# A feed-forward block whose up projection takes seven block products for eight, whose inner layer goes through DRAM, and whose down projection is a stage of its own

## The chip, the cores and the metric

One Trainium2 chip, of which the kernel uses one core. The metric is the device time of one execution in microseconds (us); shorter is better. Engines are named as in the profile: PE (matrix products), PEld (PE's weight loads, which overlap them), DVE, ACT and POOL (the three elementwise engines) and SP, whose queue issues nearly every DMA transfer.

## The reference

A whole decoder layer for 1024 tokens of 1024 channels, in float32. The change concerns its last part, a gated feed-forward block with 2816 = 22 x 128 inner channels:

```
h = rms_norm(x, pre_ffn_norm[l])
u = causal_dwconv(h @ ffn_w_up[l], ffn_conv_w[l], ffn_conv_b[l])     # 2 * 2816 columns, width 3
gate, val = jnp.split(u, 2, axis=-1)
f = (jax.nn.gelu(gate, approximate=True) * val) @ ffn_w_down[l]
x = x + rms_norm(f, post_ffn_norm[l])
```

The two products are [1024 x 1024] @ [1024 x 5632] and [1024 x 2816] @ [2816 x 1024].

## The kernel before

Everything is held with channels on the 128 partitions and tokens along the free axis, in two halves of 512 tokens. Every operand of a product is split exactly into a high and a low part (`hi`, `lo`), and each product is made of three matmuls: hi by hi, hi by lo, lo by hi. One matmul is 128x128 by 128x512. A weight tile of 128 output channels ("unit", 128x1024 for the up projection) is loaded by `load_w` (L264-271): the raw tile comes by DMA (L267), ACT makes `whi` (L269), POOL makes `wlo` (L270). `fm_unit` (L273) runs a unit, half by half: 8 blocks of 128 channels x 3 matmuls = 24 matmuls a half into one PSUM bank ("dense"; six banks).

`up(f)` (L1325-1348) makes one tile f of the inner layer from two units, u = 2f (gate) and 2f+1 (value). `conv` (L300-309) takes each bank out of PSUM: ACT writes bias + tap 0 (L303), DVE adds two shifted taps from PSUM (L307), and for the second half of the tokens two small halo operations (128x1 and 128x2, L309) bring in the last two columns of the first half (kept by a copy, L305). ACT applies gelu to the gate (L1338), DVE multiplies by the value (L1345), ACT and DVE split the result (L1346, L1347); it stays in SBUF as `mhi`, `mlo`. `down` (L1350-1360) multiplies chunks of four (one of two) inner tiles by the down weights and adds up `acc` in SBUF (L1356 on ACT for the first chunk, L1358 on DVE after). Chunks of the up projection and of the down projection alternate. The first four tiles run by halves (N_FIRST), since the second half of the tokens is still being normalised in the stage before (output projection and norms, L1264-1316). The last chunk goes by pieces of tokens, each normalised and stored at once (L1418-1441); for it x1 is loaded again in 16 transfers of 256 KB (L1387). The gelu uses another ACT table than the norms, so a table load stands behind the last gelu (L1379).

The order on each engine's queue is set by a list scheduler at build time. An engine takes its queue strictly in this order.

Of the kernel before, what the change touches and what calls it, by code (L numbers as in the profile page):

```python
# [1457 lines left out]
```

## Time and profile before

| | us |
|---|---|
| median of 3 runs (lowest to highest) | 2350.91 (2350.25 to 2351.12) |
| span of the profiled execution | 2347.0 |
| PE busy | 2261.6 |
| DVE busy | 1311.3 |
| ACT busy | 1055.4 |
| POOL busy | 912.3 |

The times are those of whole executions, the span that of the work inside one profiled execution; the difference between median and span is 3.9 us. Busy times of PE overlap: one matmul's record lasts 0.39 us, but the next one starts 0.23 us after it, so on PE the cadence of starts is the cost and not the mean record. A pause of PE shows as a value in square brackets ahead of the instruction that follows, with what ended it.

### The profile page before, as it was taken

How to read it: one execution, taken by the hardware profiler on the slowest of the kernel's cores; microseconds unless marked ns; L12 is line 12 of the kernel's file. 1: busy time of each engine (PE TensorE's matmuls, PEld its weight loads, DVE VectorE, ACT ScalarE, POOL GpSimd, SP SyncE). 2: the span in 40 equal slices, each digit the busy share in tenths (PEclk: the TensorE clock that was granted, in tenths of full speed). 3: DMA queues.
4: the chain of work that ended last, by engine and by line, in shares of the span. 5: the costliest groups of instructions: out<-in, count | busy, mean ns of one | idle time of the engine just before them, and what ended most of it. 6: DMA issues, size and time to landing. Idle time of an engine off the chain costs nothing.

```text
span 2347.0 us, 29315 instructions
## 1 busy us (share of the span) xinstructions
PE 2261.6 (96%) x11020; PEld 1828.0 (78%) x11020; DVE 1311.3 (56%) x2351; ACT 1055.4 (45%) x1842; POOL 912.3 (39%) x671
## 2 busy tenths in 40 slices
PE   8999999999999999999998999998999999999997
PEld 7997666667887788778786888876788888888886
DVE  8324875781476676565757443378714343443556
ACT  7144665666466766444443322345433131322334
POOL 4122565565233324553535264455422221222213
PEclk9999999999999999999999999998999999999998
DMA  5233112101111112021212462343221111112132
GB/s 191 81 88 96 48 40 69 57 8 59 37 54 46 46 45 72 32 77 41 77 53 83 159 202 97 117 152 111 78 63 41 59 41 50 54 32 67 46 117 72
DMA packets 90126, 173.49 MB, mean 74 GB/s; under 512 B 25280, under 2 KB 39296, under 8 KB 89984
## 3 DMA queue, kind: packets, MB, share of 16 engines
q1 hardware_dynamic: 89696, 171.39, 22.4%
q8 instruction: 87, 1.43, 0.2%
q14 instruction: 55, 0.45, 0.1%
q10 hardware_dynamic: 288, 0.22, 0.0%
HBM read 138.55 MB, written 33.03 MB: 73 GB/s over the span
## 4 chain that ended last, share of the span: by engine, by line
PE 82%; DVE 11%; ACT 3%; issue 2%; POOL 2%; DMA 1%; SPq 0%; DVEq 0%; ACTq 0%; POOLq 0%
PE dense L205 66%; PE ps_s L205 5%; PE ps_o L205 4%; PE ps_t L205 4%; PE ps_b L205 2%; DVE mx L813 2%; POOL wlo L270 1%; DVE row L307 1%; DVE o L1306 1%; ACT whi L269 0%; DVE acc L1410 0%; POOL R L1116 0%; DVE xe L1138 0%; POOL osq L1278 0%; DVE cp L733 0%
## 5 line engine op out<-in xcount | busy, mean ns | idle before, releaser
L270 POOL TENSOR_TENSOR wlo<-wraw,whi 128x1024 fp32r<-128x1024 f32 (+2 forms) x194 | 405.5, 2092 | 837.1 <-ACT whi L269 799.7
L205 PE MATMUL dense<-h_hi,whi 128*128 128x512 f32 x992 | 401.6, 405 | 3.5 <-DVE row L307 3.4
L205 PE MATMUL dense<-h_lo,whi 128*128 128x512 f32 x992 | 393.4, 397 | 0.0
L205 PE MATMUL dense<-h_hi,wlo 128*128 128x512 f32 x992 | 392.0, 395 | 0.0
L269 ACT ACTIVATE whi<-wraw 128x1024 fp32r<-128x1024 f32 (+2 forms) x194 | 179.2, 925 | 386.0 <-PE dense L205 350.2
L205 PE MATMUL dense<-hi,whi 128*128 128x512 f32 x832 | 326.6, 393 | 11.2 <-ACT whi L269 11.2
L205 PE MATMUL dense<-hi,wlo 128*128 128x512 f32 x832 | 327.0, 394 | 4.4 <-POOL wlo L270 4.3
L205 PE MATMUL dense<-lo,whi 128*128 128x512 f32 x832 | 326.0, 392 | 1.5 <-POOL lo L1313 1.5
L205 PEld LDWEIGHTS dense<-h_hi,whi 128*128 128x128 f32 x992 | 188.3, 190 | 44.4 <-ACT sa L1026 3.6
L205 PEld LDWEIGHTS dense<-h_hi,wlo 128*128 128x128 f32 x992 | 187.6, 189 | 40.0 <-issue 1.1
L205 PEld LDWEIGHTS dense<-h_lo,whi 128*128 128x128 f32 x992 | 188.3, 190 | 36.0 <-issue 1.8
L307 DVE SCALAR_TENSOR_TENSOR u<-dense,pv,u 128x511 f32<-128x511 f32 (+1 forms) x176 | 130.8, 743 | 133.3 <-ACT u L303 132.0
L853 POOL TENSOR_TENSOR wT_lo<-wT,wT_hi 128x512 fp32r<-128x512 f32 x132 | 169.2, 1292 | 86.7 <-ACT wT_hi L852 80.2
L205 PEld LDWEIGHTS dense<-hi,whi 128*128 128x128 f32 x832 | 157.5, 189 | 46.2 <-ACT whi L269 13.4
L205 PEld LDWEIGHTS dense<-hi,wlo 128*128 128x128 f32 x832 | 157.4, 189 | 40.6 <-POOL wlo L270 7.2
L205 PEld LDWEIGHTS dense<-lo,whi 128*128 128x128 f32 x832 | 157.4, 189 | 35.3 <-POOL lo L1313 2.4
L205 PE MATMUL dense<-mhi,whi 128*128 128x512 f32 x288 | 112.2, 392 | 0.3
L205 PE MATMUL dense<-mlo,whi 128*128 128x512 f32 x288 | 112.3, 390 | 0.0
L1043 POOL TENSOR_TENSOR s_lo<-sa,s_hi 128x512 fp32r<-128x512 f32 (+2 forms) x48 | 53.8, 1125 | 148.9 <-ACT s_hi L1042 137.6
L842 ACT ACTIVATE wT<-ps_s 128x512 f32<-128x512 f32 x132 | 78.4, 594 | 68.3 <-PE ps_s L205 63.6
L205 PE MATMUL dense<-mhi,wlo 128*128 128x512 f32 x288 | 105.6, 389 | 0.0
L813 DVE TENSOR_REDUCE mx<-ps_t 128x1 f32<-128x384 f32 (+3 forms) x192 | 93.9, 514 | 18.1 <-PE ps_t L205 15.9
(377 smaller groups left out, 4560.8 us busy)
## 6 DMA issues: line engine op xcount, KB each, us to landing
wraw<-in_wfm SPq DMA_DIRECT2D x62, 512.0 KB, 3.4
wraw<-in_wup SPq DMA_DIRECT2D x52, 512.0 KB, 3.3
g_d<-gate_e SPq DMA_DIRECT2D x48, 256.0 KB, 2.1
...
wraw<-in_wdn SPq DMA_DIRECT2D x32, 256.0 KB, 2.6
...
x<-in_xT SPq DMA_DIRECT2D x16, 256.0 KB, 5.5
```

Source lines behind the costliest of these rows:

```text
L205: i = f(*a, **k)
L269: act(hi, raw, AF.Copy)
L270: (V if tiles else P).tensor_tensor(lo, raw, fl(hi), op=OP.subtract)
L307: V.scalar_tensor_tensor(o[:, d:], ps[:, :512 - d], taps[d], o[:, d:], op0=OP.mult, op1=OP.add)
L813: V.tensor_reduce(mx[:, h, a, n:n + 1], pm[:, :w], axis=AX, op=OP.max)
L842: act(w.rearrange("p h q -> p (h q)"), pz, AF.Exp)
L853: P.tensor_tensor(lo, wf, fl(hi), op=OP.subtract)
L1043: (P if SB_SLO else V).tensor_tensor(s_lo[:, c0:], a[:, c0:], fl(s_hi[:, c0:]), op=OP.subtract)
L1306: i = V.scalar_tensor_tensor(o[:, j, :], o[:, j, :], pvc(PV_FFN, j), r, op0=OP.mult, op1=OP.mult)
```

## The change

The up projection keeps the first four tiles as they were, by halves. For each of the other 18 tiles, `up_pair(f)` replaces two units x two halves by a 2x2 block scheme with seven products: the contraction is cut into two halves of 512 channels (four blocks), the output into (gate unit, value unit) and the columns into the two halves of the tokens. Seven products of 4 blocks x 3 matmuls take the place of eight, 84 matmuls for 96. The token-side sums are made once (`combos`, on DVE, in place over the rows of the output projection, which are now single tiles `x`), then split into high and low parts. The weight-side sums are made for every pair in `weights7`, on POOL, and split by ACT and POOL. Results are put together in PSUM banks x, y, z with copies ("snaps") that ACT takes of unfinished sums, and additions on DVE (L1416, L1426) and POOL (L1424).

The gated inner layer is stored to DRAM (`m_d`, L1399). After the last pair the down projection runs as a stage of its own: `m_split` loads a tile (L1467), ACT and DVE split it (L1473, L1474), and five chunks follow one another. x1 is loaded by two transfers of 2 MB. The output goes out by one transfer for each tile and piece (24 for 8). Comments were emptied too, which changes nothing that runs.

```diff
-U_BUFS = 6
+U_BUFS = 4
     def lo_t(dt=R32):
-        return mp.tile([128, 512], dt, name="lo", bufs=17)
+        return mp.tile([128, 512], dt, name="lo", bufs=16)
...
+    def weights7(src0, src1, n):
+        raws = []
+        for m, src in enumerate((src0, src1)):
+            raw = (wx if turn[0] % 3 == 2 else E.wp).tile([128, 1024], F32, name="wraw", bufs=1 + (turn[0] % 3 < 2))[:, :2 * n]
+            turn[0] += 1
+            nc.sync.dma_start(raw, src)
+            raws.append(raw)
+        a11, a12, a21, a22 = [r[:, s] for r in raws for s in (slice(0, n), slice(n, 2 * n))]
...
+        act(whi, raws[0], AF.Copy)
+        P.tensor_tensor(wlo, raws[0], fl(whi), op=OP.subtract)
...
+        P.tensor_tensor(u1, a21, a22, op=OP.add)
+        P.tensor_tensor(u2, u1, a11, op=OP.add)
+        P.tensor_tensor(u4, u2, a12, op=OP.add)
+        act(h24, f24, AF.Copy)
+        P.tensor_tensor(l24, f24, fl(h24), op=OP.subtract)
+        P.tensor_tensor(u3, a11, a21, op=OP.add)
+        act(h31, f31, AF.Copy)
+        P.tensor_tensor(l31, f31, fl(h31), op=OP.subtract)
+        act(ahi, a22, AF.Copy)
+        P.tensor_tensor(alo, a22, fl(ahi), op=OP.subtract)
...
+    def snap(ps):
+        s = up_.tile([128, 512], F32, name="snap", bufs=5)
+        act(s, ps, AF.Copy)
+        return s
+    def combos(b11, b12, b21, b22, eng):
+        eng.tensor_tensor(b22, b12, b22, op=OP.subtract)
+        eng.tensor_tensor(b12, b11, b12, op=OP.subtract)
+        eng.tensor_tensor(b11, b22, b11, op=OP.subtract)
+        eng.tensor_tensor(b21, b11, b21, op=OP.add)
...
+    def gated(f, h, st):
+        V.tensor_tensor(st[0, h], st[0, h], st[1, h], op=OP.mult)
+        nc.sync.dma_start(m_d[f * 128:(f + 1) * 128, hs(h)], st[0, h])
...
+    def up_pair(f, rhs):
+        st = {}
+        w = weights7(A["wup"][2 * f], A["wup"][2 * f + 1], 512)
+        x, y, z = bank(), bank(), bank()
+        product(x, w, rhs, 1, True)
+        s1 = snap(x)
+        product(y, w, rhs, 2, True)
+        V.tensor_tensor(y, y, s1, op=OP.add)
+        conv(2 * f, 0, y, st)
+        product(x, w, rhs, 6, False)
+        s2 = snap(x)
+        product(z, w, rhs, 7, True)
+        s7 = snap(z)
+        product(x, w, rhs, 5, False)
+        s3 = snap(x)
+        P.tensor_tensor(s7, s7, s3, op=OP.subtract)
+        product(z, w, rhs, 4, False)
+        V.tensor_tensor(z, z, s2, op=OP.subtract)
+        conv(2 * f + 1, 0, z, st)
+        gated(f, 0, st)
+        product(x, w, rhs, 3, False)
+        conv(2 * f + 1, 1, s7, st)
+        conv(2 * f, 1, x, st)
+        gated(f, 1, st)
...
+    for q, k, t, place in sorted(later, key=lambda x: (-x[0], x[1])):
+        rhs[q][k] = hi, lo = place(), x_t()
+        act(hi, t, AF.Copy)
+        V.tensor_tensor(lo, t, fl(hi), op=OP.subtract)
+    for f in range(N_FIRST, NFF):
+        up_pair(f, rhs)
...
+    def m_split(f, h):
+        src = m_tile(f, h, f % 2)
+        hi, lo = hi_t(), lo_t()
+        act(hi, src, AF.Copy)
+        V.tensor_tensor(lo, src, fl(hi), op=OP.subtract)
...
+    x1s = [x1p.tile([128, 8, 512], F32, name=f"x1_{h}") for h in range(2)]
     for h in range(2):
-            nc.sync.dma_start(x1s[j][h], E.x1_d[j * 128:(j + 1) * 128, hs(h)])
+        nc.sync.dma_start(x1s[h], E.x1_d[:, hs(h)].rearrange("(a p) t -> p a t", p=128))
```

Three places of the queues matter below. The first is POOL in the middle of the up projection. Before, it holds one kind of work there, `wlo` of the next unit:

```order
L270 TENSOR_TENSOR wlo_17117<-wraw_17114,whi_17116 128x1024
L270 TENSOR_TENSOR wlo_17193<-wraw_17190,whi_17192 128x512
L270 TENSOR_TENSOR wlo_17227<-wraw_17224,whi_17226 128x512
L270 TENSOR_TENSOR wlo_17261<-wraw_17258,whi_17260 128x512
L270 TENSOR_TENSOR wlo_17295<-wraw_17292,whi_17294 128x512
```

Now one pair puts nine operations there (`uf0` and `uf1` hold u3, u1 and u2, u4; `uhi`, `ulo` their parts; `ahi`, `alo` those of one quarter of the weights; the two snaps are s7 and s3):

```order
L1349 TENSOR_TENSOR uf0_16958<-wraw_16950 128x512
L1354 TENSOR_TENSOR uf0_16958<-wraw_16948,wraw_16950 128x512
L1344 TENSOR_TENSOR wlo_17107<-wraw_17102,whi_17106 128x1024
L1350 TENSOR_TENSOR uf1_16959<-uf0_16958,wraw_16948 128x512
L1351 TENSOR_TENSOR uf1_16959<-uf1_16959,wraw_16948 128x512
L1353 TENSOR_TENSOR ulo_16963<-uf1_16959,uhi_16962 128x1024
L1424 TENSOR_TENSOR snap_16883<-snap_16883,snap_16897 128x512
L1358 TENSOR_TENSOR alo_16955<-wraw_16950,ahi_16954 128x512
L1356 TENSOR_TENSOR ulo_16961<-uf0_16958,uhi_16960 128x1024
```

Six of them are 128x512 and three 128x1024, and all read and write SBUF.

The second is ACT, in the same stretch. Before, gelu (L1338) follows the conv of its own half, and nothing behind it is wanted by the running product but the next `whi`:

```order
L303 ACTIVATE u0_18617<-dense_18618,pv_65 128x512
L1338 ACTIVATE u0_18617<-u0_18617 128x512
L269 ACTIVATE whi_18758<-wraw_18756 128x1024
L303 ACTIVATE u0_18648<-dense_18649,pv_65 128x512
L1338 ACTIVATE u0_18648<-u0_18648 128x512
```

Now two gelus, of the second half of one pair (u0_16939) and of the first half of the next (u0_17005), stand ahead of the snap of z (snap_17037, s7) that the next pair's product 4 waits for:

```order
L302 ACTIVATE u0_16939<-dense_16820,pv_65 128x512
L302 ACTIVATE u0_17005<-dense_16975,pv_65 128x512
L1343 ACTIVATE whi_17260<-wraw_17256 128x1024
L1376 ACTIVATE snap_17023<-dense_16974 128x512
L1395 ACTIVATE u0_16939<-u0_16939 128x512
L1395 ACTIVATE u0_17005<-u0_17005 128x512
L1376 ACTIVATE snap_17037<-dense_16976 128x512
```

The gelus themselves wait for DVE's taps, so a snap now waits for DVE by way of the queue. DVE's queue up to the second of them is:

```order
L1426 TENSOR_TENSOR dense_16822<-dense_16822,snap_16869 128x512
L304 COPY halo_16913<-dense_16822 128x2
L306 SCALAR_TENSOR_TENSOR u1_16914<-dense_16822,pv_65,u1_16914 128x511
L306 SCALAR_TENSOR_TENSOR u1_16933<-snap_16883,pv_65,u1_16933 128x511
L308 SCALAR_TENSOR_TENSOR u1_16933<-halo_16913,pv_65,u1_16933 128x1
L306 SCALAR_TENSOR_TENSOR u1_16914<-dense_16822,pv_65,u1_16914 128x510
L306 SCALAR_TENSOR_TENSOR u1_16933<-snap_16883,pv_65,u1_16933 128x510
L308 SCALAR_TENSOR_TENSOR u1_16933<-halo_16913,pv_65,u1_16933 128x2
L1398 TENSOR_TENSOR u0_16851<-u0_16851,u1_16914 128x512
...
L306 SCALAR_TENSOR_TENSOR u0_17005<-dense_16975,pv_65,u0_17005 128x510
```

Between the last two shown stand the taps of u0_16939 (two from PSUM and two from its halo), a halo copy and the first tap of u0_17005.

The third place is SP's queue where the up projection ends. Before, x1 comes in pieces of 128x512 between loads of weights:

```order
L267 DMA wraw_19279<-in_wdn4 128x256
L1387 DMA hi_19419<-x1_d_73 128x512
L1387 DMA hi_19423<-x1_d_73 128x512
L1387 DMA lo_19420<-x1_d_73 128x512
L267 DMA wraw_19307<-in_wdn4 128x256
```

Now each half of x1 is one transfer, and the first one stands ahead of the loads of the inner layer's tile 0 (u0_18351, u0_18357), the second ahead of tiles 2 and 3:

```order
L1467 DMA u1_18363<-m_d_14865 128x512
L1467 DMA u1_18369<-m_d_14865 128x512
L1517 DMA x1_0_19931<-x1_d_73 128x8x512
L1467 DMA u0_18351<-m_d_14865 128x512
L1467 DMA u0_18357<-m_d_14865 128x512
L1517 DMA x1_1_19932<-x1_d_73 128x8x512
L266 DMA snap_19905<-in_wdn5 128x512
L1399 DMA m_d_14865<-u0_18237 128x512
L1467 DMA u1_18387<-m_d_14865 128x512
L1399 DMA m_d_14865<-u0_18325 128x512
```

On ACT the table load and the first `m_split` now stand behind the last gelu, so the down projection's first operand is made after it:

```order
L302 ACTIVATE u0_18325<-dense_18206,pv_65 128x512
L1395 ACTIVATE u0_18325<-u0_18325 128x512
L1492 ACT_TABLE_LOAD
L1473 ACTIVATE hi_18353<-u0_18351 128x512
L1473 ACTIVATE hi_18359<-u0_18357 128x512
L1473 ACTIVATE hi_18365<-u1_18363 128x512
```

Before, the table load had the last chunks of the down projection beside it:

```order
L1346 ACTIVATE mhi_19186<-u0_19086 128x512
L1379 ACT_TABLE_LOAD
L269 ACTIVATE whi_19309<-wraw_19307 128x256
L269 ACTIVATE whi_19337<-wraw_19335 128x256
```

What was behind the gelu there were weights of matmuls that had inner tiles in SBUF; now it is the inner tiles themselves.

A fourth place is the first pair. On ACT its second snap (snap_15637, s2) stands behind the gelu of its own first half:

```order
L302 ACTIVATE u0_15619<-dense_15589,pv_65 128x512
L1343 ACTIVATE whi_15874<-wraw_15870 128x1024
L1395 ACTIVATE u0_15619<-u0_15619 128x512
L1376 ACTIVATE snap_15637<-dense_15588 128x512
```

That gelu's taps stand on DVE behind eight splits of token-side sums (L1458, the first and the last of them shown) and the taps of the last unit before the pairs (u1_15474):

```order
L1458 TENSOR_TENSOR x_15531<-x_14450,hi_15530 128x512
...
L1458 TENSOR_TENSOR x_15559<-x_14049,lo_15558 128x512
L306 SCALAR_TENSOR_TENSOR u1_15474<-dense_15449,pv_65,u1_15474 128x511
L308 SCALAR_TENSOR_TENSOR u1_15474<-halo_15166,pv_65,u1_15474 128x1
L306 SCALAR_TENSOR_TENSOR u1_15474<-dense_15449,pv_65,u1_15474 128x510
L308 SCALAR_TENSOR_TENSOR u1_15474<-halo_15166,pv_65,u1_15474 128x2
L1416 TENSOR_TENSOR dense_15589<-dense_15589,snap_15603 128x512
L1398 TENSOR_TENSOR u0_15436<-u0_15436,u1_15474 128x512
L304 COPY halo_15618<-dense_15589 128x2
L306 SCALAR_TENSOR_TENSOR u0_15619<-dense_15589,pv_65,u0_15619 128x511
L306 SCALAR_TENSOR_TENSOR u0_15619<-dense_15589,pv_65,u0_15619 128x510
```

Before there was nothing of this kind: the units with both halves simply follow the four tiles that run by halves.

PE's queue in a steady pair D, with E the pair after it, is (product, and its number of matmuls): 6 of D 12, 7 of D 2, 1 of E 12, 2 of E 9, 7 of D 10, 5 of D 12, 2 of E 3, 4 of D 12, 3 of D 12; 84 in all. In the whole program PE has 216 matmuls fewer (18 pairs x 12), all of the form 128x128 by 128x512.

## Rows read from the trace of the kernel before

**Rows 1.** The page, first part: busy time of each engine, its share of the span, instructions.

```profile
PE 2261.6 (96%) x11020; PEld 1828.0 (78%) x11020; DVE 1311.3 (56%) x2351; ACT 1055.4 (45%) x1842; POOL 912.3 (39%) x671
```

**Rows 2.** Busy time by stretch: start and end in us, length, then busy us and instructions of each engine, TensorE's granted clock, DMA share and GB/s. The FFN fills 1700 to 2280 and has its first tiles ahead of that.

```profile
1500.00:1600.00 100.00, 91.79 (x384) 73.15 (x383) 68.02 (x58) 45.89 (x70) 53.25 (x23) 0.97 0.38 133
1600.00:1700.00 100.00, 91.06 (x376) 71.45 (x375) 81.62 (x107) 48.99 (x69) 49.09 (x22) 0.97 0.30 100
1700.00:2200.00 500.00, 499.73 (x2201) 412.79 (x2200) 190.85 (x315) 140.05 (x196) 115.37 (x62) 1.00 0.16 50
2280.00:2347.00 67.00, 51.87 (x327) 46.34 (x325) 42.32 (x90) 27.20 (x58) 18.96 (x20) 0.90 0.18 64
```

**Rows 3.** Groups of instructions between 1700 and 2200 us, POOL: line, engine, operation, tiles, shapes and count, then busy us and mean ns of one, then the idle time before and what ended it.

```profile
L270 POOL TENSOR_TENSOR wlo<-wraw,whi 128x1024 fp32r<-128x1024 f32 x32 | 76.8, 2399 | 234.0 <-ACT whi L269 234.0
L270 POOL TENSOR_TENSOR wlo<-wraw,whi 128x512 fp32r<-128x512 f32 x30 | 38.6, 1292 | 154.0 <-ACT whi L269 154.0
```

**Rows 4.** The same view and stretch, ACT.

```profile
L303 ACT ACTIVATE u<-dense,pv 128x512 f32<-128x512 f32 x60 | 46.1, 768 | 31.6 <-PE dense L205 31.6
L269 ACT ACTIVATE whi<-wraw 128x1024 fp32r<-128x1024 f32 x32 | 34.0, 1061 | 71.9 <-PE dense L205 71.9
L1338 ACT ACTIVATE u<-u 128x512 f32<-128x512 f32 x30 | 19.0, 633 | 63.8 <-DVE u L309 37.9 <-DVE u L307 25.9
L269 ACT ACTIVATE whi<-wraw 128x512 fp32r<-128x512 f32 x30 | 18.6, 630 | 94.9 <-PE dense L205 94.9
L1356 ACT ACTIVATE acc<-dense 128x512 f32<-128x512 f32 x15 | 8.8, 589 | 16.6 <-PE dense L205 16.6
```

**Rows 5.** The same view and stretch, DVE. L307 and L305 read PSUM, L1358 one operand of PSUM and one of SBUF, the others SBUF alone.

```profile
L307 DVE SCALAR_TENSOR_TENSOR u<-dense,pv,u 128x511 f32<-128x511 f32 x60 | 44.7, 745 | 102.4 <-ACT u L303 102.4
L1358 DVE TENSOR_TENSOR acc<-acc,dense 128x512 f32<-128x512 f32 x48 | 32.7, 687 | 88.6 <-PE dense L205 88.6
L309 DVE SCALAR_TENSOR_TENSOR u<-halo,pv,u 128x1 f32<-128x1 f32 x30 | 28.3, 943 | 0.0
L1345 DVE TENSOR_TENSOR u<-u,u 128x512 f32<-128x512 f32 x29 | 20.1, 692 | 1.0
L309 DVE SCALAR_TENSOR_TENSOR u<-halo,pv,u 128x2 f32<-128x2 f32 x29 | 6.0, 206 | 0.0
L305 DVE COPY halo<-dense 128x2 f32<-128x2 f32 x30 | 4.8, 159 | 98.6 <-ACT u L303 98.6
```

**Rows 6.** The timeline between 1880 and 1884 us, POOL and DVE: start, duration, engine, line, operation, tiles, and in brackets the idle time before with what ended it.

```profile
1880.88 2.40 POOL L270 TENSOR_TENSOR wlo<-wraw,whi 128x1024 fp32r<-128x1024 f32 x1 [8.49 <-ACT whi L269]
...
1881.50 0.75 DVE L307 SCALAR_TENSOR_TENSOR u<-dense,pv,u 128x511 f32<-128x511 f32 x1 [4.16 <-ACT u L303]
...
1882.17 1.13 DVE L309 SCALAR_TENSOR_TENSOR u<-halo,pv,u 128x1 f32<-128x1 f32 x1
...
1883.22 0.74 DVE L307 SCALAR_TENSOR_TENSOR u<-dense,pv,u 128x510 f32<-128x510 f32 x1
```

**Rows 7.** Groups between 1480 and 1700 us, where DVE and POOL both work on SBUF: the POOL operations and one of DVE's splits.

```profile
L1315 DVE TENSOR_TENSOR lo<-o,hi 128x512 fp32r<-128x512 f32 x8 | 9.0, 1129 | 0.0
...
L1300 POOL TENSOR_TENSOR o<-o,ox 128x512 f32<-128x512 f32 x4 | 7.0, 1739 | 6.1 <-DVE o L1298 6.1
```

**Rows 8.** The timeline of PE around the pauses in the norm before the FFN. The last three rows are matmuls behind a single pause.

```profile
1585.67 0.50 PE L205 MATMUL dense<-hi,whi 128*128 128x512 f32 x1 [3.66 <-ACT whi L269]
...
1588.33 0.79 PE L205 MATMUL dense<-hi,wlo 128*128 128x512 f32 x1 [1.92 <-POOL wlo L270]
1588.92 0.63 PE L205 MATMUL dense<-hi,whi 128*128 128x512 f32 x1
...
1593.18 0.43 PE L205 MATMUL dense<-lo,whi 128*128 128x512 f32 x1
...
1649.62 0.50 PE L205 MATMUL dense<-hi,whi 128*128 128x512 f32 x1 [2.19 <-ACT whi L269]
...
1650.64 0.39 PE L205 MATMUL dense<-hi,whi 128*128 128x512 f32 x1
1650.87 0.39 PE L205 MATMUL dense<-lo,whi 128*128 128x512 f32 x1
```

**Rows 9.** Busy time by stretch once more, five microseconds in which the transfers of x1 run.

```profile
2270.00:2275.00 5.00, 5.00 (x24) 4.15 (x23) 3.60 (x6) 1.45 (x3) 1.48 (x2) 1.00 1.02 374
```

**Rows 10.** The DMA issues of the whole program: tiles, queue, number, KB each, median us from issue to landing; loads of 256 KB and those of x1.

```profile
wraw<-in_wdn SPq DMA_DIRECT2D x32, 256.0 KB, 2.6
...
hi<-x_d SPq DMA_DIRECT2D x8, 256.0 KB, 4.8
```

**Rows 11.** The timeline of ACT from 2268 to 2278 us, with the last table load and a weight split that waited for its load; and of SP, the issue of that load.

```profile
2269.32 1.28 ACT L1379 ACT_TABLE_LOAD   x1
2270.62 0.42 ACT L269 ACTIVATE whi<-wraw 128x256 fp32r<-128x256 f32 x1
...
2277.12 0.42 ACT L269 ACTIVATE whi<-wraw 128x256 fp32r<-128x256 f32 x1 [3.35 <-DMA wraw<-in_wdn]
...
2272.16 0.33 SPq L267 DMA_DIRECT2D wraw<-in_wdn  x1
```

More of the change, by code (lines that the diff above doesn't have):

```diff
@@ L1265, in tail_stage, with x_t @@
     up_ = es.enter_context(tc.tile_pool(name="up", side="right", reuse_waits="tile", bufs=U_BUFS))
+    op2 = es.enter_context(tc.tile_pool(name="o", reuse_waits="tile", bufs=1))
+    def x_t(dt=R32):
+        return op2.tile([128, 512], dt, name="x", bufs=26)
     op = ExitStack()
     ow = op.enter_context(tc.tile_pool(name="ow", reuse_waits="tile", bufs=2))
+    rows = []
     for h in range(2):
-        o = ow.tile([128, 8, 512], F32, name="o")
+        o = [x_t(F32) for _ in range(8)]
+        rows.append(o)
         def sumsq(sums, src, eng=V):
@@ new lines, in product, with bank @@
+    def product(ps, w, rhs, q, first):
+        hi, lo = w[q]
+        for k, b in enumerate(rhs[q]):
+            s = slice(k * 128, (k + 1) * 128)
+            for n, (x, y) in enumerate(((hi, b[0]), (hi, b[1]), (lo, b[0]))):
+                mm(ps, x[:, s], y, start=first and k == 0 and n == 0, stop=k == len(rhs[q]) - 1 and n == 2,
+                   skip_group_check=True)
+    def bank():
+        return psd.tile([128, 512], F32, name="dense", tag="dense")
+    def snap(ps):
+        s = up_.tile([128, 512], F32, name="snap", bufs=5)
+        act(s, ps, AF.Copy)
+        return s
@@ new lines, in combos, with conv @@
+    def combos(b11, b12, b21, b22, eng):
[3 more added lines that the diff above has]
+        eng.tensor_tensor(b21, b11, b21, op=OP.add)
+    m_d = E.scratch("m_d", [NFF * 128, T])
+    def conv(u, h, ps, st):
+        s = u % 2
+        if h == 0:
+            st["halo", s] = up_.tile([128, 4], F32, name="halo", bufs=12)
+        st[s, h] = up_.tile([128, 512], F32, name=f"u{s}")
+        E.conv(st[s, h], h, ps, [pvc(PV_FW, 3 * u + 2 - d) for d in range(3)], pvc(PV_FB, u), st["halo", s])
+        if s == 0:
+            act(st[0, h], st[0, h], AF.Gelu_apprx_tanh)
@@ new lines, in tail_stage @@
+    first = [{} for _ in range(N_FIRST)]
+    for h in range(2):
+        for f, st in enumerate(first):
+            up_half(f, h, st)
+    rhs = {q: [None] * 4 for q in range(1, 8)}
+    later = []
+    for k in range(4):
+        quarters = [(1, h2[0, k]), (2, h2[0, k + 4]), (3, h2[1, k + 4])]
+        lows = [rows[0][k], rows[1][k], rows[0][k + 4], rows[1][k + 4]]
+        combos(*lows, V)
+        for q, b in quarters:
+            rhs[q][k] = b
+        t2, t1, t4, t3 = lows
+        for q, t in ((6, t2), (7, t3)):
+            rhs[q][k] = hi, lo = x_t(), x_t()
+            act(hi, t, AF.Copy)
+            V.tensor_tensor(lo, t, fl(hi), op=OP.subtract)
+        later += [(5, k, t1, hi_t), (4, k, t4, lo_t)]
@@ new lines, in tail_stage, with w_split @@
+    for ci, (f0, nf) in enumerate(DOWN[:last]):
+        if ci == 0:
+            acc = [[x_t(F32) for _ in range(8)] for _ in range(2)]
+        down(ci, f0, nf)
+    f0, nf = DOWN[last]
+    ms = [[None, None] for _ in range(nf)]
+    ws = []
+    def w_split(j, place):
+        ws.append(load_w(A[f"wdn{last}"][j], 512, place, up_.tile([128, 512], F32, name="snap", bufs=5)))
+    for k in range(nf):
+        ms[k][0] = m_split(f0 + k, 0)
+    for j in range(4):
+        w_split(j, (x_t(), x_t()))
@@ L1390, in tail_stage @@
+    for k in range(nf):
+        ms[k][1] = m_split(f0 + k, 1)
+    for j in range(4, 8):
+        w_split(j, (hi_t(), lo_t()))
+    wx_.close()
+    x1p = es.enter_context(tc.tile_pool(name="x1", reuse_waits="tile", bufs=1))
+    x1s = [x1p.tile([128, 8, 512], F32, name=f"x1_{h}") for h in range(2)]
+    for h in range(2):
+        nc.sync.dma_start(x1s[h], E.x1_d[:, hs(h)].rearrange("(a p) t -> p a t", p=128))
     ended = None
@@ L1422, in tail_stage @@
         for j in range(8):
-            ps = psd.tile([128, 512], F32, name="dense", tag="dense")
+            ps = bank()
             hi, lo = ws[j]
```

139 lines of the change are left out of this document (59 added, 80 removed).

## The prediction

> **What bounds the kernel now.** I read the page's busy times first: PE is busy 2261.6 us of a span of 2347.0 [rows 1], so the kernel is bound by PE nearly everywhere. Then the stretches [rows 2]: from 1700 to 2200 us, inside the FFN, PE has 499.73 of 500 us at a granted clock of 1.00, and 2201 matmuls, one every 0.2272 us. DVE, ACT and POOL work for 191, 140 and 115 us of these 500. So a matmul that is taken out there saves its whole 0.2272 us, as long as the three others, with much work added, still deliver in time. The reader should keep the two stretches before in mind, 91 to 92 us of PE's 100 with DVE at 68 to 82 [rows 2]: where the work of DVE and POOL gets dense, PE does wait.
>
> **Part 1, fewer matmuls.** 216 matmuls of the form that fills the FFN go: 216 x 0.2272 = -49.1 us. A pair takes 84 x 0.2272 = 19.1 us for 21.8. This term is the surest; all others are costs.
>
> **Part 2, the work of a pair beside PE.** ACT: three splits of 128x1024 at 1.06, one of 128x512 at 0.63, four snaps at 0.59 (a copy out of PSUM), four convs at 0.77, two gelus at 0.63 [rows 4]: 3.18 + 0.63 + 2.36 + 3.07 + 1.27 = 10.5 us of 19.1. DVE: eight taps at 0.745, two additions in PSUM at 0.69, two products at 0.69, two halo copies at 0.16, four halo taps at 0.20 [rows 5]: 9.9 us of 19.1. POOL: three operations of 128x1024 at 2.40 and six of 128x512 at 1.29 [rows 3]: 14.9 us of 19.1. Taken alone, each hides beneath PE. The loads stay 1 MB a pair and the stores add 1 MB, at stretches with a DMA share of 0.16 [rows 2]; I cost them at nothing, and PE's cadence covers them unless a queue's order holds them up (part 5).
>
> DVE and POOL are not independent. A POOL operation ran from 1880.88 to 1883.28; DVE's tap from PSUM ran beside it at its normal 0.75, but the 128x1 halo tap behind it, which has its operands in SBUF, ended only at 1883.30, after 1.13 us [rows 6]. Over the stretch that form has a mean of 943 ns, while the 128x2 one, which often comes when POOL is done, has 206 [rows 5]. In the norm, POOL's 128x512 takes 1.74 for 1.29, DVE's split 1.13 for 0.69 [rows 3, 5, 7]. So operations of DVE that use only SBUF wait for POOL's to end, and the other way round. Of these a pair has eight: two taps of s7 (which is a copy in SBUF), four halo taps, two products; 1.5 + 0.8 + 1.4 = 3.7 us. POOL's 14.9 and these 3.7 together take 18.6 of 19.1 us. It fits, with half a microsecond left. The Trainium skill says the same in SBUF — State Buffer (section Who interferes with whom): DVE and GpSimd (POOL) share one pair of ports, an exclusive lock that one instruction holds to its end. By that rule the two would take turns to fill 18.6 us; the row of 1.13 us agrees.
>
> **Part 3, the chain through DVE in a steady pair.** Product 4 adds to bank z, so it has to wait for snap s7, which ACT takes only after two gelus; the second gelu wants DVE's last tap of the new pair's first half. Take T as the end of product 3 of the pair before. PE then has 60 matmuls until product 4: s7 is wanted at T + 13.6. DVE's chain begins when product 4 of the pair before ends, at T - 2.7, and goes through 16 operations: one addition (0.69), six taps (4.5), four halo taps (0.8), two halo copies (0.3), a product (0.7) and two more taps of the new half (1.5): 8.5 us. Without any waiting the gelu could start at T + 5.8 and nothing is late. But seven of them use SBUF alone. POOL's mean operation is 14.9 / 9 = 1.66 us; if each of the seven meets a working POOL, it waits between nothing and that. I take 1.07 each, some two thirds of it, since POOL's next operation is queued already when DVE's comes (7.5 in all): T + 13.3. Gelu 0.63 and snap 0.59, with some hand-over, give T + 14.65, and PE waits 1.05. One small halo tap that gets in between two POOL operations takes that away. So I count half of it, 0.55 us in 17 pairs: **+9.4** (bounds 0, and 17 x 1.05 = 18 for every pair; with all seven at the whole 1.66, T + 17.5, 5.3 us a pair, which is the rival below). A pause of this length shouldn't lower PE's cadence: one of 2.19 us was followed, a microsecond on, by starts 0.23 us apart [rows 8].
>
> **Part 4, the start of the pairs.** Eight token-side splits at 1.13 (contended) [rows 7], the last unit's taps (1.9, and 1.3 of waiting), addition, product, copy, two taps (3.0) stand on DVE ahead of the gelu that stands ahead of the first pair's snap s2. The splits can begin some 1.7 us before PE begins the pair: 9.0 + 3.2 + 3.0 - 1.7, then two gelu-length steps (1.2), say 15 us after that begin; PE wants the snap after 48 matmuls, 10.9: 4.4 us of waiting. Uncontended splits at 0.69 [as L1345 in rows 5] would give 0.9. Weight sums of the first pairs come late on ACT and POOL because both are still splitting token tiles: one ACT split with its POOL part behind is 1.06 + 2.40 = 3.5 [rows 3, 4], I take 4 for both. And pauses of 3.66 and 1.92 us were followed by some ten matmuls at 0.43 instead of 0.23 us [rows 8], +2.1. Sum **+10.5** (bounds 4 and 18).
>
> **Part 5, from up to down.** Before, chunks alternate and PE doesn't pause. Now the first chunk wants inner tiles from DRAM. Let T be the last product's end. ACT: conv 0.77, then DVE's four taps (1.9), gelu 0.63, table load 1.28 [rows 4, 5, 11]: T + 4.7, then 0.63 for the first split: T + 5.3 at least. But the loads of tile 0 stand on SP's queue behind 2 MB of x1, issued when product 4 ends, T - 2.7. In the trace, transfers of x1 filled the engines at 374 GB/s [rows 9], their own 256 KB took 4.8 for 2.6 us to land [rows 10], and a split waited 3.35 us for its load issued at 2272.16 among them, ready at 2277.1 [rows 11]: so later loads wait behind. 2 MB at 374 GB/s is 5.6 us, T + 2.9; two tiles of 256 KB 1.4, landing 2.6: T + 7. Split: PE begins at about T + 8. The second 2 MB stands ahead of tiles 2 and 3, behind tile 0: T + 4.3 + 5.6, then six transfers of 256 KB (4.2), landing and split (3.2): T + 17. PE has 24 matmuls until then, so it pauses again or runs them at the lower cadence; the other 24 of the first two units end at T + 24. Without the stage cut 48 matmuls would end at T + 10.9: **+13.5** (bounds: 6, if the transfers share and only the chain over ACT counts; 18, with the lower cadence in both pauses).
>
> **Part 6, the rest.** The first four tiles keep their matmuls and the tail its pieces; 67 us from 2280 on with 51.9 of PE [rows 2]. 24 output transfers for 8, and 128x512 tiles: nothing, at most 1 us either way.
>
> Sum, against the profiled span: 2347.0 - 49.1 + 9.4 + 10.5 + 13.5 = 2331.3, with the 3.9 us around the span 2335 us, 0.7% below 2350.9.
>
> **The rivals.** (a) The waits hide: gelus and snaps come in time in nearly every pair (0 for 9.4), the start costs 4, the cut 9: 2347 - 49.1 + 13 + 3.9 = 2315. For it: every engine alone is below 80% of a pair. Against: the port's 18.6 of 19.1. (b) Each pair waits 1.05, and start and cut stand at 14 and 18: 2347 - 49.1 + 18 + 14 + 18 + 3.9 = 2352, no change. For it: queues are taken strictly in order, and part 3 repeats identically. (c) Slower: the port between DVE and POOL becomes the bound. If POOL's operations take the contended 1.74 (and 2.84 for 128x1024 by the same 0.44 added) [rows 3, 7], they need 6 x 1.74 + 3 x 2.84 = 19.0 us, and if DVE's 3.7 come on top of that, 22.7 us a pair: 18 x (22.7 - 19.1) = 65 in the place of 9.4, so 2391. It decides the sign at 21.8 less what start and cut cost, about 20.5 us of port time a pair. Against: 0.44 is most likely just the DVE operation that POOL waited for, and then it is counted twice. (d) That the change doesn't take matmuls away is excluded: PE's queue has 216 fewer.
>
> **How the numbers follow.** Forecast 0.47, (a) 0.17, (b) 0.20, (c) 0.16. A measurement of this kernel can tell about 0.2%, 4.7 us, from no change: faster is below 2346, slower above 2356. The forecast's own bounds from parts 3 to 5 (0 to 18, 4 to 18, 6 to 18, where 33.4 is taken) give 2312 to 2356 with all ends together, which is unlikely; half of it each way is 2323 to 2346. Faster: 0.47 and 0.17 less a little = 0.63; same: 0.20; slower: 0.17. The range leaves out the end of (a) and nearly all of (c): 2313 to 2360.
>
> **What would show it.** Matmuls per pair 84 at a cadence of 0.227 between pauses; POOL 14.9 us a pair or more, with DVE's taps of s7 longer than 0.75; pauses of PE of about a microsecond ahead of product 4, ended by ACT's snap, in about half of the pairs; a pause of about 8 us at the cut, ended by a split of `m_d`, and a second; some pauses in the first pair. It would be wrong if PE pauses ahead of other products (weights from POOL late: then the port is the bound), if the granted clock drops in the pairs, or if the loads of the cut don't wait behind x1.

## The result and the profile after

The changed kernel takes 2334.43 us (median of 4 runs, 2332.65 to 2336.55) against 2350.58 for the kernel before beside it: a ratio of 0.9932, 95% interval [0.9918, 0.9946]. The prediction said 2335. The profiled span is 2331.9 us, the sum said 2331.3. But the sum is right because errors of opposite sign cancel, as the stretches show.

The page's first part and the stretches of the changed kernel (the columns as in [rows 2]):

```profile
PE 2221.6 (95%) x10804; PEld 1790.9 (77%) x10804; DVE 1415.1 (61%) x2419; ACT 1126.2 (48%) x1966; POOL 1120.3 (48%) x797
...
1600.00:1700.00 100.00, 85.78 (x340) 66.25 (x339) 89.83 (x117) 48.83 (x68) 56.19 (x23) 0.91 0.35 116
1700.00:1800.00 100.00, 94.38 (x411) 76.52 (x410) 73.92 (x89) 48.44 (x70) 85.28 (x48) 1.00 0.23 74
1800.00:2000.00 200.00, 200.00 (x884) 165.61 (x883) 138.13 (x188) 104.45 (x150) 166.43 (x95) 1.00 0.24 83
2000.00:2100.00 100.00, 84.12 (x351) 67.14 (x350) 52.73 (x79) 45.52 (x73) 41.01 (x26) 0.93 0.50 171
```

In the pairs PE is busy all the time (200.00 of 200.00), although POOL now works 83 us of 100. The pauses are at the two ends of the pairs, in the stretches from 1600 to 1800 and from 2000 to 2100 us; in two of these three the granted clock is lower too (0.91 and 0.93; 1.00 from 1700 to 1800). The timeline of PE there, matmuls that began after a pause (the bracket: length of the pause, and what ended it):

```profile
1667.75 0.79 PE L204 MATMUL dense<-hi,wlo 128*128 128x512 f32 x1 [4.96 <-POOL wlo L269]
...
1709.14 0.50 PE L204 MATMUL dense<-x,uhi 128*128 128x512 f32 x1 [1.35 <-ACT uhi L1352]
...
1722.84 0.50 PE L204 MATMUL dense<-hi,uhi 128*128 128x512 f32 x1 [1.99 <-ACT snap L1376]
...
1730.06 0.50 PE L204 MATMUL dense<-hi,uhi 128*128 128x512 f32 x1 [1.49 <-ACT snap L1376]
...
2041.12 0.50 PE L204 MATMUL dense<-hi,uhi 128*128 128x512 f32 x1 [0.23 <-ACT snap L1376]
...
2047.63 0.50 PE L204 MATMUL dense<-lo,ahi 128*128 128x512 f32 x1 [1.23 <-ACT snap L1376]
...
2063.94 2.33 PE L204 MATMUL dense<-hi,whi 128*128 128x512 f32 x4 [10.55 <-ACT hi L1473]
...
2073.92 2.08 PE L204 MATMUL dense<-hi,whi 128*128 128x512 f32 x4 [2.68 <-ACT hi L1473]
```

Between 1730.06 and 2041.12 there is none. To put a price on each stretch I cut the span at three matmuls: the last of the norm's row sums before the second half is normalised, the first product of sums (1709.14, the 263rd matmul after it; the kernel before has the same 263 there), and the last matmul of the pairs (2053.00), which only the changed kernel has. The cadence in the pairs is 0.2267 us, so 216 matmuls are 49.0 us.

| stretch | before | after | after, against before without the 216 | predicted |
|---|---|---|---|---|
| up to the last row sums | 1631.96 | 1630.92 | -1.0 | 0 |
| to the first product of sums | 67.59 | 78.22 | +10.6 | start: +10.5 |
| pairs, 1488 matmuls (337.3 at the cadence) | | 343.86 | +6.5: +4.5 in the first two, +2.0 in the last | loop: +9.4 |
| the rest, from the last product to the end | 647.44 with the pairs | 278.90 | +17.8 | cut: +13.5 |
| sum with -49.0 | 2347.0 | 2331.9 | -15.1 | -15.7 |

The third entry for "the rest" is 278.90 - (647.44 - 49.0 - 337.3). With the pauses of the first two pairs counted to the start, the start cost 15.1, the loop 2.0, and the cut 17.8. That the table has +10.6 beside +10.5 is chance: the 10.5 were forecast for waits of the first pair and its weights, most of which come behind 1709.14 or just ahead of it, and most of the 10.6 lies ahead of them.

The steady pair itself. Some groups of the changed kernel from 1740 to 2030 us (columns as in [rows 3]):

```profile
L306 DVE SCALAR_TENSOR_TENSOR u<-snap,pv,u 128x510 f32<-128x510 f32 x15 | 41.9, 2791 | 0.0
L308 DVE SCALAR_TENSOR_TENSOR u<-halo,pv,u 128x2 f32<-128x2 f32 x31 | 35.7, 1152 | 0.0
L306 DVE SCALAR_TENSOR_TENSOR u<-dense,pv,u 128x511 f32<-128x511 f32 x47 | 34.6, 737 | 0.0
L1354 POOL TENSOR_TENSOR uf<-wraw 128x512 f32<-128x512 f32 x16 | 28.0, 1747 | 0.0
L1398 DVE TENSOR_TENSOR u<-u,u 128x512 f32<-128x512 f32 x31 | 26.4, 851 | 1.9 <-ACT u L1395 0.4
L1350 POOL TENSOR_TENSOR uf<-uf,wraw 128x512 f32<-128x512 f32 x16 | 20.7, 1295 | 0.0
L308 DVE SCALAR_TENSOR_TENSOR u<-halo,pv,u 128x1 f32<-128x1 f32 x31 | 12.6, 406 | 0.0
L306 DVE SCALAR_TENSOR_TENSOR u<-snap,pv,u 128x511 f32<-128x511 f32 x15 | 11.5, 770 | 0.2 <-ACT u L302 0.2
```

Taps from PSUM keep 0.74 us. Of the operations in SBUF alone, the second tap of s7 takes 2.79 for 0.74 and the 128x2 halo tap 1.15 for 0.20, while the first tap of s7 (0.77) and the 128x1 halo (0.41) hardly wait. POOL's nine operations take 16.1 us a pair by their means, 1.2 more than the 14.9 counted.

### The profile page after: what moved, and what is told of

Its sections match the earlier page's. It is cut to its first block, busy times and chain, and to the rows that moved or that the text cites. A ratio compares the mean times of both kernels' runs of the same rounds, so it can differ in the third digit from the quotient of the medians.

```text
span 2331.9 us, 29572 instructions
## 1 busy us (share of the span) xinstructions
PE 2221.6 (95%) x10804; PEld 1790.9 (77%) x10804; DVE 1415.1 (61%) x2419; ACT 1126.2 (48%) x1966; POOL 1120.3 (48%) x797
## 3 DMA queue, kind: packets, MB, share of 16 engines
q8 instruction: 85, 1.39, 0.2%
## 4 chain that ended last, share of the span: by engine, by line
PE 78%; DVE 12%; issue 5%; ACT 2%; POOL 2%; DMA 0%; DVEq 0%; POOLq 0%; ACTq 0%
PE dense L204 62%; PE ps_s L204 6%; PE ps_o L204 4%; PE ps_t L204 4%; PE ps_b L204 2%; DVE mx L812 2%; POOL wlo L269 1%; DVE row L306 1%; DVE x L1313 1%; DVE x L1540 0%; DVE osq L1285 0%; ACT whi L268 0%; DVE xe L1137 0%; POOL wlo L1344 0%; POOL R L1115 0%
## 5 line engine op out<-in xcount | busy, mean ns | idle before, releaser
L269 POOL TENSOR_TENSOR wlo<-wraw,whi 128x1024 fp32r<-128x1024 f32 (+2 forms) x158 | 328.8, 2082 | 547.6 <-ACT whi L268 538.2
L268 ACT ACTIVATE whi<-wraw 128x1024 fp32r<-128x1024 f32 (+2 forms) x158 | 141.4, 895 | 324.6 <-PE dense L204 288.2
L204 PE MATMUL dense<-hi,whi 128*128 128x512 f32 x688 | 272.9, 399 | 24.5 <-ACT hi L1473 13.2
L204 PE MATMUL dense<-hi,wlo 128*128 128x512 f32 x688 | 268.1, 399 | 9.4 <-POOL wlo L269 8.8
L204 PE MATMUL dense<-lo,whi 128*128 128x512 f32 x688 | 271.5, 395 | 1.7 <-DVE lo L1322 0.9
L204 PEld LDWEIGHTS dense<-hi,wlo 128*128 128x128 f32 x688 | 131.5, 191 | 41.1 <-POOL wlo L269 11.5
L204 PE MATMUL dense<-x,uhi 128*128 128x512 f32 x360 | 117.0, 390 | 1.6 <-ACT uhi L1352 1.3
L306 DVE SCALAR_TENSOR_TENSOR u<-dense,pv,u 128x510 f32<-128x510 f32 (+1 forms) x140 | 101.9, 737 | 6.5 <-ACT u L302 6.4
L812 DVE TENSOR_REDUCE mx<-ps_t 128x1 f32<-128x384 f32 (+3 forms) x192 | 94.0, 514 | 18.5 <-PE ps_t L204 16.3
L1489 DVE TENSOR_TENSOR x<-x,dense 128x512 f32<-128x512 f32 x64 | 43.8, 686 | 86.7 <-PE dense L204 86.6
L851 ACT ACTIVATE wT_hi<-wT 128x512 fp32r<-128x512 f32 x132 | 82.2, 629 | 13.9 <-POOL wT L843 12.2
```

The costliest lines, as they stand in the source:

```text
L204: i = f(*a, **k)
L268: act(hi, raw, AF.Copy)
L269: (V if tiles else P).tensor_tensor(lo, raw, fl(hi), op=OP.subtract)
L306: V.scalar_tensor_tensor(o[:, d:], ps[:, :512 - d], taps[d], o[:, d:], op0=OP.mult, op1=OP.add)
L812: V.tensor_reduce(mx[:, h, a, n:n + 1], pm[:, :w], axis=AX, op=OP.max)
L851: act(hi, wf, AF.Copy)
```

## The experiments

Times are compared by their ratio to the kernel before on the same chip, and by the three stretches of the table, since the part ahead of the last row sums, at which no experiment aims, differs by up to 6 us from profile to profile (1627.4 to 1633.3). Runs without a ratio were executed once, so for them only the profile's stretches are compared.

**x1 later.** Both transfers of x1 are held behind a load of inner tiles (the last of the fourth chunk of the down projection; the expectation says the second).

```diff
+        loads.append(nc.sync.dma_start(t, m_d[f * 128:(f + 1) * 128, hs(h)]))
...
+    with tc.issue_after(loads[31].ins):
         for h in range(2):
             nc.sync.dma_start(x1s[h], ...)
```

> The two transfers of x1 are issued only behind the loads of the inner tiles of the second down chunk; nothing else changes. In the changed kernel PE pauses 10.55 us between the last product and the down projection, and the load of inner tile 0 was issued 0.4 us behind the first 2 MB of x1. Theory (loads wait behind x1): tile 0 is then issued at about the same time but lands some 2.6 us later instead of 9, its split stands ahead of the last gelu, and the pause falls to 4 to 6 us, the whole kernel by 5 to 10 us (2325 to 2330). Rival (the chain conv, taps, gelu, table load on ACT sets the restart): the pause stays above 9 us and the time within 2 us of 2334.

Ratio 0.9889 [0.9874, 0.9904], 2323.96 us. The rest fell from 278.90 to 270.8, the other stretches stayed within 0.5 us. The chain at the cut, ACT and SP of the changed kernel:

```profile
2057.57 0.63 ACT L1395 ACTIVATE u<-u 128x512 f32<-128x512 f32 x1 [3.37 <-DVE u L308]
2058.22 1.28 ACT L1492 ACT_TABLE_LOAD   x1
2063.26 2.35 ACT L1473 ACTIVATE hi<-u 128x512 fp32r<-128x512 f32 x4 [3.76 <-DMA u<-m_d]
...
2047.56 4.20 SPq L266 DMA_DIRECT2D snap<-in_wdn  x4
...
2052.80 0.38 SPq L1517 DMA_DIRECT2D x<-x_d  x1
2053.23 1.63 SPq L1467 DMA_DIRECT2D u<-m_d  x2
```

Tile 0's loads, issued 0.4 us behind x1, kept ACT waiting until 2063.26, ten microseconds, and 3.76 after the table was in. x1 itself was issued only at 2052.80, behind weight loads that SP's queue held until 2051.76. With x1 later, ACT and PE:

```profile
2056.72 2.36 ACT L1474 ACTIVATE hi<-u 128x512 fp32r<-128x512 f32 x4 [3.95 <-DMA u<-m_d]
...
2057.40 2.34 PE L204 MATMUL dense<-hi,whi 128*128 128x512 f32 x4 [5.45 <-ACT hi L1474]
```

The pause is 5.45 for 10.55, the second one (2.68) is gone, and the splits stand ahead of the last gelu and of the table load. The loads did wait behind x1; the rival is out.

**Loads first.** x1 is held as above, and the loads of the last chunk's weights are held behind inner tiles too (the last of the second chunk).

```diff
+        with tc.issue_after(loads[15].ins):
             ws.append(load_w(A[f"wdn{last}"][j], 512, place, ...))
```

> As the run with x1 later, and the loads of the last down chunk's weights too stand behind the first inner tiles, so that no other load is ahead of those on SP's queue. Theory (SP's queue in order is the whole of the cut): the first tiles are in SBUF before the last product ends, the pause falls under 2.5 us and the time by 12 to 18 us (2316 to 2322). Rival (only the 2 MB matter, the weight loads don't): as the run with x1 later, within 2 us of it. Second rival (ACT and DVE, which have the last pair's taps to do first): the pause stays at 4 us or more.

Ratio 0.9885 [0.9871, 0.9898], 2323.03 us; run again beside other kernels:

> The kernel with the first inner tiles' loads ahead of x1 and of the last weights, once more, beside the two others of this call: 2320 to 2326, about 1 us below the one with x1 later if the weight loads matter at all, a ratio to the kernel before of 0.987 to 0.990.

0.9878 [0.9864, 0.9891], 2321.77. The first inner tiles are now in SBUF in time, and PE pauses 1.39 us:

```profile
2051.15 1.48 PE L204 MATMUL dense<-hi,whi 128*128 128x512 f32 x4 [1.39 <-ACT hi L1474]
2053.73 0.80 PE L204 MATMUL dense<-lo,whi 128*128 128x512 f32 x1 [1.09 <-DVE lo L1475]
...
2067.35 0.50 PE L204 MATMUL dense<-hi,whi 128*128 128x512 f32 x1 [1.81 <-ACT whi L268]
```

(These rows are of the first run.) But the rest is 269.3 and 269.1 in the two runs, only 1.5 to 1.8 below the run with x1 later. What the first pause lost came back behind it: a split of DVE, then weights of the next units that ACT makes behind the splits. By the pause the theory was right, by the time the first rival: holding x1 back takes away some 8 of the cut's 17.8 us, the weight loads some 1.5 more.

**Eight products in the same stage.** All 18 tiles with eight products, `m_d` and the down stage kept.

```diff
-    rhs = {q: [None] * 4 for q in range(1, 8)}
...
-        up_pair(f, rhs)
...
+            w = load_w(A["wup"][u], 1024)
+            for h in range(2):
+                ps, = fm_unit(psd, w, lambda k, h: h2[h, k], 8, halves=(h,))
+                conv(u, h, ps, st)
```

> Eight products instead of seven (each unit by both halves with its whole contraction, as before), but with the inner layer in DRAM and the down projection as a stage of its own. No sums, snaps or weight sums. Theory (the 216 matmuls are worth 49 us, the start of the pairs costs some 15 and the cut some 19): the kernel before plus the cut, 2350.6 + 15 to 21 = 2365 to 2372. Rival (the cut's cost belongs to the seven products, since the last pair's chain is what delays it): 2351 to 2358.

Ratio 1.0053 [1.0039, 1.0067], 2361.47 us: between the two. Without the weight sums' buffers x1 found room early, at the beginning of the up projection, and a weight split waited for its load there (SP and ACT of that run):

```profile
1653.95 1.00 SPq L1506 DMA_DIRECT2D x<-x_d  x2
...
1668.52 1.06 ACT L268 ACTIVATE whi<-wraw 128x1024 fp32r<-128x1024 f32 x1 [6.36 <-DMA wraw<-in_wup]
```

If so, x1's transfers held up something else. With x1 behind the loads of inner tiles, as above:

> Eight products with the inner layer in DRAM and the down stage of its own, and x1's two transfers behind the loads of the second down chunk. In the run with eight products x1's transfers were issued at the beginning of the up projection and a weight load came 8 us late behind them. Theory (that pause of 3.67 us with its slow matmuls was x1's doing; the stage alone costs 5 to 6 us): 2355 to 2359, so that seven products in the same stage are worth 33 to 37 us of the 49. Rival (the pause has another cause): 2361 to 2364 as before.

1.0014 [1.0006, 1.0023], 2354.48 us, a bit under the theory's range. The stretch to the 263rd matmul is 66.53 us (74.01 with x1 early, 67.59 before), and the rest with the up projection 656.09 for 647.44: by the stretches the separate down stage costs 8.7 us with x1 behind the fourth chunk, close to the 8 that stay with seven products (269.1 - 261.1), and 5.6 in the run with x1 early (the rest there is 653.0). The pause of 3.67 us is gone, so it was x1's doing. By the profiled spans the whole kernel is 6.4 us above the kernel before, by the ratio only 0.14%, some 3 us; its executions range over 9 us.

Which kernel with seven products stands in an equal stage? The one with x1 later, 0.9889 (on another chip, against the kernel before there): 1.25%, 29 us. Beside the eight products stands the one with the loads first, 0.9878: 1.36%, 32 us, but that one holds the last weights back as well. So seven products instead of eight are worth 29 to 32 of 49.0 us in this stage, give or take some 4 by the intervals; 17 to 20 are lost, by the stretches at the two ends of the pairs.

**POOL fuller.** The split that makes l31 runs twice, or three times, in every pair.

```diff
         P.tensor_tensor(l31, f31, fl(h31), op=OP.subtract)
+        P.tensor_tensor(l31, f31, fl(h31), op=OP.subtract)
```

> The changed kernel with one more POOL operation of 128x1024 in every pair (l31 is computed twice into the same place), 2.4 us more on POOL. Theory of the prediction (POOL and DVE's SBUF-only operations fill 18.6 of 19.1 us of a shared port, so 21.0 is too much): pairs grow by 1 to 2 us, 18 to 36 in all, with pauses of PE in every pair. Rival (POOL's idle time in a pair, about a sixth in the trace of the changed kernel, some 3 us, really is room): pairs keep their 19.1 us and the span stays within 4 us of 2332.

> The same with two more POOL operations of 128x1024 in every pair, 4.8 us. Theory of a port that is full at 19.1: port time is 14.9 + 3.7 + 4.8 = 23.4 us, pairs grow by about 4.3 us, 77 in all, to a span near 2409. Rival (an idle share of 3 us is room and only the rest counts): 1.8 us a pair, 32 in all, span near 2364.

One more (executed once): a span of 2341.4 us, the pairs 352.90 for 343.86. That is outside the rival's 4 us, but not where the theory put it. In the steady pairs PE stays busy; POOL is at 95%:

```profile
1800.00:1900.00 100.00, 100.00 (x438) 81.66 (x438) 81.47 (x95) 50.97 (x71) 95.12 (x52) 1.00 0.23 79
```

A steady pair takes 19.22 us for 19.04, so some 6 of the 9 us are in the first and the last pairs. POOL's ten operations take 18.5 us a pair by their means, again 1.2 more than they need alone (14.9 + 2.4). Two more (executed once): 2401.7 us, the pairs 416.96, so 73 us more. The steady pairs take 22.7 us on average, 3.7 more; the rest is again in the first and the last ones. In every pair there is a pause of PE, as in these two, one behind the other:

```profile
1929.57 0.50 PE L204 MATMUL dense<-x,ulo 128*128 128x512 f32 x1 [2.33 <-POOL ulo L1358]
...
1952.85 0.50 PE L204 MATMUL dense<-x,ulo 128*128 128x512 f32 x1 [2.33 <-POOL ulo L1358]
```

The 73 us are near the theory's 77, but this doesn't show a full port: POOL's own eleven operations need 14.9 + 4.8 = 19.7 us, more than the 19.04 of a pair, with no DVE at all (by their means they take 21.0). Of the 3.7 us the pause is 2.33; the stretch from 1900 to 2000 us has a granted clock of 0.96 besides. What the runs do show is that a port filled to 18.6 of 19.1 us could not have taken 2.4 more for 0.2: it had more than 2 us of room, not 0.5.

**The start.** Where do the 4.96 us that PE pauses ahead of 1667.75 come from? The chain of waits of the changed kernel (start, duration, what) has one split of POOL there that takes three times its 2.40:

```profile
1660.47 7.24 POOL wlo L269
```

DVE's timeline has what ran beside it:

```profile
1660.58 0.68 DVE L1384 TENSOR_TENSOR x<-x 128x512 f32<-128x512 f32 x1
1661.19 0.68 DVE L1382 TENSOR_TENSOR x<-x 128x512 f32<-128x512 f32 x1
...
1664.20 1.28 DVE L1383 TENSOR_TENSOR x<-x 128x512 f32<-128x512 f32 x2
1665.40 0.74 DVE L306 SCALAR_TENSOR_TENSOR u<-dense,pv,u 128x511 f32<-128x511 f32 x1
1666.06 1.65 DVE L308 SCALAR_TENSOR_TENSOR u<-halo,pv,u 128x1 f32<-128x1 f32 x1
```

Eight sums and splits run in one piece, none of them waits, and POOL's split ends 2.3 us after the start of the first tap from PSUM (1665.40), about its own length; the halo tap behind that now waits in its turn. This isn't how the two always meet. In the same trace DVE runs eight splits in one piece from 1699.97 on, and POOL's operations get in between them (DVE's first four, then POOL):

```profile
1699.97 6.88 DVE L1458 TENSOR_TENSOR x<-x,hi 128x512 fp32r<-128x512 f32 x4
...
1702.87 1.73 POOL L1350 TENSOR_TENSOR uf<-uf,wraw 128x512 f32<-128x512 f32 x1
1704.57 1.74 POOL L1358 TENSOR_TENSOR alo<-wraw,ahi 128x512 fp32r<-128x512 f32 x1
```

There both take turns: 1.7 us for POOL's 1.29, and 6.88 for four splits that take 0.68 alone. What decides between the two cases no run shows. First the sums are left out:

```diff
-        combos(*lows, V)
```

> The 16 token-side sums are left out (the products take the rows as they are), so the output is not the reference's; all splits stay. Theory (DVE's run of SBUF-only sums keeps POOL's weight split from the port at the start): the pause of 4.96 us with the slow matmuls behind it goes, 5 to 9 us less than the changed kernel's span of 2331.9. Rival (the weights are late on ACT, or by the splits that stay): less than 3 us.

Executed once: the pause is gone, and the stretch to the first product of sums fell from 78.22 to 71.67, 6.5 us. The span of 2329.0 is only 2.9 below, which by itself would be the rival; but the part ahead of the last row sums, where nothing was changed, was 1.3 us longer, and the rest 2.3, with a pause of 11.78 at the cut. So the sums cost the start 6.5 of its 10.6 us. Then they went to POOL:

```diff
-        combos(*lows, V)
+        combos(*lows, P)
```

> The 16 token-side sums go to POOL instead of DVE. In the changed kernel one weight split of POOL, 2.4 us elsewhere, took some 7 us while DVE ran SBUF-only sums one behind the other, and PE paused 4.96 us for it. Theory (DVE's run of sums keeps POOL from the port): POOL's order then gives the weight splits their turn, that pause goes, and the excess of the start falls by 4 to 8 us (2326 to 2331). Rival (POOL is simply the later engine there; 16 sums at 1.29 us are 21 us more for it): weights come later still, PE pauses more, and the time rises by 3 to 15 us (2337 to 2349).

Ratio 0.9957 [0.9944, 0.9969], 2340.05 us, the stretch 82.90: the rival. POOL's queue has sums ahead of the weight splits, and PE still pauses 4.71, with 1.48 and 1.80 later. Then, over the kernel with the loads first (stretch 77.7 to 78.0), the sums in groups (`marks` are the gating products):

```diff
+        with tc.issue_after(marks[2 + k].ins):
             combos(*lows, V)
```

> The kernel with the first inner tiles' loads ahead of x1 and of the last weights, and the four groups of token-side sums (four operations each) held behind the gating products of four tiles, so that they come in groups with the convs' work between instead of in one run. Theory (one run of sums keeps POOL from the port, groups don't): the pause of 4.96 us falls below 2 and the time by 4 to 8 us against that kernel's 2323 (2315 to 2319). Rival (sums and splits come later, and the first pairs wait for them by as much): within 2 us of 2323.

Ratio 0.9898 [0.9881, 0.9914], 2324.22 us: the rival. The pause of 4.96 is 1.95, but others of 1.27, 1.14 and 2.68 came; the stretch is 79.83. Last, a small copy out of PSUM behind each sum:

```diff
+                last = eng.tensor_tensor(o, x, y, op=op)
+            with tc.issue_after(last.ins):
+                last = eng.tensor_copy(room[:, :2], kept[-1][:, :2])
```

> The kernel with the first inner tiles' loads ahead, and behind each of the 16 token-side sums a copy of 128x2 out of PSUM on DVE (0.15 us, its result is not used). Theory (POOL gets the shared port only when DVE's next operation doesn't want it, and a run of SBUF-only sums never lets it in): with a PSUM operation behind each sum POOL's weight split starts within a sum's length; the pause of 4.96 us falls below 1.5, the stretch from the last norm's row sums to the first product of sums from 77.7 to 70 to 74 us, the time to 2315 to 2319. Rival (POOL now takes its turn at every break, DVE's sums take twice as long, and the first pairs wait for them): that stretch stays above 76 us, the time within 2 us of 2323.

Ratio 0.9894 [0.9879, 0.9910], 2327.18 us, the stretch 80.08. The pause is as the theory had it; the stretch is the rival's, and the time lies 2 us above even the rival's range. The chain of waits of this kernel:

```profile
1662.44 3.09 POOL wlo L269
```

The timelines of DVE and ACT:

```profile
1663.23 0.14 DVE L1390 COPY room<-psn 128x2 f32<-128x2 f32 x1
1663.30 5.55 DVE L1458 TENSOR_TENSOR x<-x 128x512 fp32r<-128x512 f32 x2
...
1677.25 0.63 ACT L1457 ACTIVATE x<-x 128x512 fp32r<-128x512 f32 x1 [4.56 <-DVE x L1388]
1677.78 1.04 ACT L268 ACTIVATE whi<-wraw 128x1024 fp32r<-128x1024 f32 x1
```

POOL's split gets in at the copy and takes 3.09 for 7.24 us; PE's pause there is 0.82. (That the copy let it in is likely and not shown: the operations behind the copy are splits like those of 1699.97, between which POOL got in without one.) But then DVE's two splits take 5.55 us, the sums come later, and ACT, whose queue has splits of these sums ahead of the next `whi`, hands the delay to PE at 1678.87 (1.41) and 1681.54 (1.93). Three orders moved PE's wait, and none made the stretch shorter (79.8 to 82.9 us).

## Why the prediction was right, point by point

**Part 1** held: 216 matmuls, a cadence of 0.227, 49.0 us.

**Part 2**: the work beside PE hides, as forecast, with the counts as given (POOL 14.9 counted, 16.1 measured). But 18.6 of 19.1 us for the port was wrong, and with it the rule that the two take turns for their whole durations. The sum added DVE's 3.7 us whole; what they cost POOL is 1.2 us a pair, and 2.4 us of further POOL work fitted into the steady pair but for 0.2: 14.9 + 2.4 + 3.7 = 21.0 us of work in 19.22, so the two overlap in part.

**Part 3** is the term that was mis-sized: 9.4 forecast, 2.0 measured, and all of that in the last pair; 0 in the steady ones. The place was right: in the last pair product 4 waits 1.23 for s7. In a steady pair, with T at 1904.27 (DVE, POOL, ACT, PE):

```profile
1905.77 2.56 DVE L306 SCALAR_TENSOR_TENSOR u<-snap,pv,u 128x510 f32<-128x510 f32 x1
1908.25 1.25 DVE L308 SCALAR_TENSOR_TENSOR u<-halo,pv,u 128x2 f32<-128x2 f32 x1
...
1905.38 2.40 POOL L1356 TENSOR_TENSOR ulo<-uf,uhi 128x1024 fp32r<-128x1024 f32 x1 [0.87 <-ACT uhi L1355]
1907.86 1.62 POOL L1349 TENSOR_TENSOR uf<-wraw 128x512 f32<-128x512 f32 x1
...
1913.72 1.29 ACT L1395 ACTIVATE u<-u 128x512 f32<-128x512 f32 x2 [4.30 <-DVE u L308]
1914.92 0.58 ACT L1376 ACTIVATE snap<-dense 128x512 f32<-128x512 f32 x1
...
1917.87 0.39 PE L204 MATMUL dense<-lo,ahi 128*128 128x512 f32 x1
```

s7 is ready at T + 11.2, product 4 begins at T + 13.6 (1917.87), as worked out. I had 14.65. The seven operations waited some 4.3 us, not 7.5: two of them (the second tap of s7, above, and the last halo tap) meet an operation of POOL of 2.4 us, the others meet its gaps or short ones. "Two thirds of POOL's mean operation" for each was the step that failed; the margin is 2.4 us.

**Part 4**, the start: 10.5 forecast, 15.1 measured. The waits that it named are there and smaller: s2 behind a gelu 1.99 for 4.4, weight sums 0.58, 1.35 and 0.22 for 4. Without the token-side sums the start is 71.67 - 67.59 + 4.5 = 8.6 us, near the forecast. What the prediction missed is POOL: it looked for DVE waiting on POOL, and here POOL waits on DVE's run of sums, before the pairs begin, at weights of the tiles by halves, which is worth 6.5 us. It had bounds of 4 and 18, by which the range held.

**Part 5**, the cut: 13.5 forecast, 17.8 measured. The mechanism is shown: taking x1 out of the way gave 8.1 us. The first pause was sized 8 and is 10.55. From x1's issue to tile 0's landing the sum had 9.7 us, the trace has 10.4 (2052.80 to 2063.23); but x1 was issued at T - 0.6, behind weight loads on SP's queue, and not at T - 2.7 (T is 2053.39). The second pause is 2.68. I had also taken the loss without x1 as about 6; the runs with x1 behind say 8 to 10.

**The rivals**: (a) was right on the loop and wrong on start and cut; (b) was wrong on the loop. (c), the port as the bound, is excluded by the steady pairs; where it would begin is open, since with 4.8 us more in each POOL alone is too slow already. The errors of parts 3 (-7.4), 4 (+4.6) and 5 (+4.3), with -1.0 ahead of the FFN, add up to 0.5 us: that the number was hit this closely is luck. The 3.9 us around the span are no constant either: each execution of these kernels takes 1.7 to 2.2 us more than its span, and the profiled one of the kernel before was some 2 us faster than the median.

What stays open: which loads made the pause at the cut differ from 9.8 to 11.8 us between profiles, what decides whether POOL gets in between DVE's operations, and whether an order exists in which the start costs less with the sums in it; three orders didn't.
